# A hybrid decoder layer on one core: the last gate of the attention branch and the mask multiplications take other places in the program

## The chip, the cores and the metric

The kernel runs on one core of one Trainium2 chip. The metric is the device time of one execution in microseconds (us), as the median of several runs; lower is better. The engines are named as in the profile: PE is TensorE (matmuls; PEld its weight loads), DVE is VectorE, ACT is ScalarE, POOL is GpSimd, and SP is the queue that issues most DMAs. A name with a q behind it (ACTq, SPq) is an engine's queue that issues a DMA or handles a semaphore.

## The reference

One layer on a sequence of 1024 tokens of width 1024: a SwiGLU half-step, a mixing sub-layer with two branches, and a second SwiGLU half-step. The change lies in the mixing sub-layer:

```python
h = rms_norm(x, mix_norm[l])
z = h @ w_in[l]
q, k, v, qi, ki, wi, u, g_attn, g_pool = jnp.split(z, SPLIT_POINTS, axis=-1)
q = apply_rope(rms_norm(q.reshape(B, S, N_HEADS, HEAD_DIM), q_norm[l]), cos_h, sin_h)
k = apply_rope(rms_norm(k, k_norm[l]), cos, sin)
...
y_attn = dsa_attention(q, k, v, qi, ki, wi, topk)
y_pool = multiscale_pool(u, pool_w[l], pool_b[l], pool_scale[l])
merged = (jax.nn.sigmoid(g_attn) * (y_attn @ proj_attn[l])
          + jax.nn.sigmoid(g_pool) * (y_pool @ proj_pool[l]))
x = x + merged @ w_out[l]
```

`g_attn` and `g_pool` have 1024 channels each. The top 256 keys of a query are found by a bitwise search for the 256th largest score; what comes out is a mask over the keys, one for each block of 128 queries.

## The kernel before

Everything stands in one program in the order in which it is written; each engine works through its own part in that order and waits at semaphores for the others. Two arenas of on-chip memory, `fa` and `ra`, hold all buffers, so most operands in the profile bear these two names. PSUM is a ring of four slots (`ps()`).

**Units.** The columns of `w_in` for u, g_attn and g_pool are 20 tiles of 128 channels, "units" 0 to 19 here. `unit(u)` computes one by 48 matmuls of 512 columns (fp32 as a pair of high and low part: weight high by input high, high by low, low by high, in this order for each of eight row tiles). The weights are split on the way: ACT casts the high part (line 135), POOL subtracts it to get the low part (line 141). `next_unit(u)` runs unit u and then issues the split of unit u+2. Units 8 to 15 are the pooling branch's gates: in each turn e of that loop a unit, its sigmoid on ACT (line 995), a product of 24 matmuls, and a multiplication on DVE that reads that product from PSUM (`self.dve(... stage[e % 2] ...)`, recorded under line 119). Units 16 to 19 are gates 4 to 7 of the attention branch: `gate_out` takes the sigmoid (line 919) into a buffer and stores it to `d_gate` (line 920). For gates 4, 5 and 6 this buffer is `stage[1]`, which first has to be stored to `d_pool[7]` by the SP queue (line 1016).

**The search.** `topk()` is a generator of DVE and ACT work that is spread between the units by an estimate of the two engines' times (`pump`). At its end six masks are made, one each for query blocks 2 to 7, by four DVE instructions each (lines 865, 867, 869, 871), and ACT multiplies each mask by 1e30 (`A.mul`, lines 874 and 875). In the program's order the end of the search lies in the turns of units 14 to 17, so DVE, which lags behind, still runs it after PE has gone on.

**QKV.** Two weight tiles of 320 columns, `cd[0]` and `cd[1]`, are split inside the loop of gates 4 to 6: `cd[0]` (one cast and one subtraction of 2560 elements per row) at gate 4, `cd[1]` (1920 and 640) at gate 5. Then eight blocks follow, "N0" to "N7" here: 48 matmuls of 320 columns (`narrow`), a copy and a square on ACT (lines 1033, 1034), norm and rope on DVE and POOL (`qkv_norm`, from a reduction under line 119 to line 666), the leaving copies on ACT and POOL (`qkv_leave`, lines 1052, 1055, 1056) and a transposition on PE (`qkv_turn`, line 1062). Gate 7 (unit 19) stands behind N7. Behind it come the last `qkv_leave` and the attention loop, whose first instructions are matmuls of 128 columns on PE and an addition with a minimum on DVE for each head. DVE comes to these only when the norm of N7 is done, since that stands ahead in its order.

Of the kernel before, what the change touches and what calls it, by code (L numbers as in the profile page):

```python
# [16 lines left out]
NB = S // 128  # L17
# [10 lines left out]
BIG = 1e30  # L28
# [30 lines left out]
class Block:  # L59
# [28 lines left out]
    def f(self, kib, *shape):  # L88
        return self.cut(self.fa, self.F_END, kib, shape)
# [610 lines left out]
    def mix(self, nback):  # L700
        nc = self.nc
        A, V, P = nc.scalar, nc.vector, nc.gpsimd
# [10 lines left out]
        Ss, o = {}, 6.0  # L713
# [3 lines left out]
        Wk = f(22.5, 1024)  # L717
# [21 lines left out]
        def unit(u):  # L739
            z = self.ps()  # L740
            s = ring[u % 3]
            self.wide(z, s[:, 0], s[:, 1], self.h, ND)
            return flat(z)
# [63 lines left out]
        def topk():  # L807

            key, cand, cnt, got, least, val, up = (st[:, 6 * j:6 * j + 6] for j in range(7))
            bits = lambda t: t.bitcast(I32)
            part = lambda t, g: t[:, 3 * g:3 * g + 3]
            one = lambda t, g, k: t[:, 3 * g + k:3 * g + k + 1]
            cost = lambda b: 80 + 1.1 * 128 * (b + 1)
            n_of = lambda b: (b + 1) * 128

            def count(g, thr, op):
                for k, b in enumerate(groups[g]):  # L820
                    V.tensor_scalar(junk[0][:, 0:n_of(b)], Ss[b], one(thr, g, k) if thr is not None else 0.0, None,  # L821
                                    op0=op, op1=OP.add, accum_out=one(cnt, g, k))
                    yield cost(b)

            for k, b in enumerate(groups[0]):
                V.memset(one(least, 0, k), 2.0 * TOPK - 0.5 - n_of(b))
            V.memset(part(least, 1), TOPK - 0.5)
            for g in range(2):
                yield from count(g, None, OP.is_ge)

            V.tensor_scalar(bits(got), cnt, TOPK - 0.5, None, op0=OP.is_lt)
            V.tensor_scalar(bits(key), bits(got), 31, 31, op0=OP.logical_shift_left, op1=OP.arith_shift_right)
            V.tensor_scalar(bits(part(key, 0)), bits(part(key, 0)), -2147483648, None, op0=OP.bitwise_xor)
            yield 600
            for bit in range(30, -1, -1):
                V.tensor_scalar(bits(cand), bits(key), 1 << bit, None, op0=OP.bitwise_xor)  # L836
                for k, b in enumerate(groups[0]):
                    A.activation(junk[1][:, 0:n_of(b)], Ss[b], AF.Sign, bias=one(cand, 0, k), accum_out=one(cnt, 0, k))  # L838
                yield 400
                yield from count(1, cand, OP.is_ge)  # L840
                V.tensor_tensor(bits(got), cnt, least, op=OP.is_ge)
                V.scalar_tensor_tensor(bits(key), bits(got), bit, bits(key), op0=OP.logical_shift_left,
                                       op1=OP.bitwise_xor)
                yield 900
            V.tensor_scalar(bits(part(val, 0)), bits(part(key, 0)), -2147483648, None, op0=OP.bitwise_xor)
            V.tensor_copy(part(val, 1), part(key, 1))

            yield from count(0, val, OP.is_gt)
            v0, u0, g0 = part(val, 0), part(up, 0), part(got, 0)
            V.scalar_tensor_tensor(u0, v0, -1.0, v0, op0=OP.mult, op1=OP.max)  # L850
            V.scalar_tensor_tensor(u0, u0, 1.2 * 2.0 ** -24, v0, op0=OP.mult, op1=OP.add)
            V.tensor_scalar(bits(g0), part(cnt, 0), TOPK - 0.5, None, op0=OP.is_ge)
            V.copy_predicated(v0, bits(g0), u0)
            yield 300
            for g in (0, 1):
                yield from count(g, val, OP.is_gt)

            V.tensor_scalar(cnt, cnt, -1.0, float(TOPK), op0=OP.mult, op1=OP.add)
            for b in range(2, NB):
                g = 0 if b in groups[0] else 1  # L860
                k = groups[g].index(b)
                n = n_of(b)
                sc, eq, cum = Ss[b], junk[0][:, 0:n], junk[1][:, 0:n]
                v = one(val, g, k)
                V.tensor_scalar(eq, sc, v, None, op0=OP.is_equal)
                yield cost(b)
                V.tensor_tensor_scan(cum, eq, eq, 0.0, op0=OP.add, op1=OP.bypass)
                yield cost(b)
                V.scalar_tensor_tensor(cum, cum, one(cnt, g, k), eq, op0=OP.is_gt, op1=OP.mult)
                yield cost(b)  # L870
                V.scalar_tensor_tensor(sc, sc, v, cum, op0=OP.is_lt, op1=OP.max)
                yield cost(b)
                if b > 2:
                    A.mul(Ss[b - 1], Ss[b - 1], BIG)
            A.mul(Ss[NB - 1], Ss[NB - 1], BIG)


        u32 = [f(54, 1024), f(58, 1024)]
# [39 lines left out]
        def gate_out(e, z, buf):  # L918
            A.activation(buf, z, AF.Sigmoid)
            nc.scalar.dma_start(self.d_gate[e], buf)  # L920
            self.pump()
# [29 lines left out]
        self.split(pws[:, 0], pws[:, 1], pwraw, "pool")  # L951
        window(0)
        self.bg = topk()


        def next_unit(u):
            z = unit(u)
            split_unit(u + 2)
            return z
# [43 lines left out]
            if e == 4:  # L1003
                nc.sync.dma_start(rawCD[0], winv[:, :, 0:320])

        for e in range(4, 7):
            if e == 4:
                self.split(cd[0][0], cd[0][1], rawCD[0], "pool")
                for k, c in enumerate(parts):
                    nc.sync.dma_start(rawCD[1 + k], winv[:, c, 320:640])  # L1010
            if e == 5:
                for k, c in enumerate(parts):
                    self.split(cd[1][0][:, c], cd[1][1][:, c], rawCD[1 + k], "pool")
            z = next_unit(12 + e)
            if e == 4:
                nc.sync.dma_start(self.d_pool[held], stage[held % 2])
            gate_out(e, z, stage[1])
# [32 lines left out]
        def qkv_leave(b):  # L1050
            t1 = sets[b % 2][1]
            A.mul(qnat[:, b], t1[:, 0:8], -0.125)
            kk = t1[:, 8:9].to_broadcast([128, 2, 64])
            kb = khl[b % 2]
            A.copy(rr(kb[:, 0]), kk)
            P.tensor_tensor(kb[:, 1], kk, kb[:, 0], op=OP.subtract)
            self.split(vS[:, b, 0], vS[:, b, 1], zcd[b % 2][:, 576:640], "pool")
# [135 lines left out]
            self.pump()  # L1193
        while self.bg is not None:
            self.bg_step()
        gate_out(7, unit(19), Wk)
        qkv_leave(NB - 1)
        qkv_turn(NB - 2, quarters()[:, 0])

# [335 lines left out]
```

## Time and profile before

| | |
|---|---|
| three runs | 2055.8, 2056.26, 2056.49 us (median 2056.26) |
| the profiled execution | 2057.76 us, of which the span is 2055.9 us |
| PE busy | 1980.2 us, 96% of the span |
| DVE busy | 1455.2 us, 71% |
| ACT busy | 864.8 us, 42% |
| POOL busy | 243.2 us, 12% |

The span is the time from the first to the last instruction that the profiler recorded; the rest of the execution's time lies around it. Times within the profile count from the span's start. The part that matters lies between 1000 and 1145 us: units 16 to 18, the end of the search, N0 to N7, unit 19 and the start of attention. A row of the timeline is a run of like instructions on one engine, with its start, its length, the count, and in brackets how long the engine was idle before it and whose end released it. PE's clock has two levels here, 1.2 and 2.4 GHz; PEclk 0.50 is the lower, 1.00 the upper.

### The profile page before, as it was taken

How to read it: one execution, taken by the hardware profiler on the slowest of the kernel's cores; microseconds unless marked ns; L12 is line 12 of the kernel's file. 1: busy time of each engine (PE TensorE's matmuls, PEld its weight loads, DVE VectorE, ACT ScalarE, POOL GpSimd, SP SyncE). 2: the span in 40 equal slices, each digit the busy share in tenths (PEclk: the TensorE clock that was granted, in tenths of full speed). 3: DMA queues.
4: the chain of work that ended last, by engine and by line, in shares of the span. 5: the costliest groups of instructions: out<-in, count | busy, mean ns of one | idle time of the engine just before them, and what ended most of it. 6: DMA issues, size and time to landing. Idle time of an engine off the chain costs nothing. (4 is left out here: it accounts for less than half of the span.)

```text
span 2055.9 us, 26096 instructions
## 1 busy us (share of the span) xinstructions
PE 1980.2 (96%) x9449; PEld 1656.4 (81%) x9449; DVE 1455.2 (71%) x2464; ACT 864.8 (42%) x1437; POOL 243.2 (12%) x260
## 2 busy tenths in 40 slices
PE   8999999999999989999979898998999999999999
PEld 7788888888888877888778787787788888888887
DVE  6887777777566476788956895546787777776554
ACT  6423323333454455677423884124423323333332
POOL 0000000000000332122134654210000000000000
PEclk9999999999999999999999999999999999999999
DMA  4355454458684202022210014331255454458665
GB/s 134 103 186 183 161 167 144 164 203 313 208 274 139 67 21 72 31 92 78 76 43 11 1 51 162 137 113 53 91 181 188 158 170 144 164 200 317 194 216 173
DMA packets 167056, 287.02 MB, mean 140 GB/s; under 512 B 12160, under 2 KB 78224, under 8 KB 166928
## 3 DMA queue, kind: packets, MB, share of 16 engines
q1 hardware_dynamic: 163088, 271.73, 39.4%
q10 hardware_dynamic: 3744, 13.63, 1.7%
q8 instruction: 74, 1.21, 0.2%
q14 instruction: 54, 0.44, 0.1%
q0 software_dynamic: 96, 0.01, 0.0%
HBM read 200.91 MB, written 84.41 MB: 139 GB/s over the span
## 5 line engine op out<-in xcount | busy, mean ns | idle before, releaser
L316 PE MATMUL psum<-ra 128*128 128x512 f32 (+1 forms) x5688 | 1276.3, 386 | 11.2 <-DVE fa L502 4.3
L316 PEld LDWEIGHTS psum<-ra 128*128 128x128 f32 x5688 | 1053.9, 188 | 230.2 <-issue 5.8
L108 PE MATMUL psum<-ra 128*128 128x512 f32 (+5 forms) x3112 | 639.6, 363 | 39.0 <-POOL ra L141 12.7
L108 PEld LDWEIGHTS psum<-ra 128*128 128x128 f32 x3112 | 529.3, 191 | 128.0 <-ACT fa L795 17.4
L426 ACT CAST ra<-fa 128x512 fp32r<-128x512 f32 x280 | 168.9, 617 | 303.6 <-PE psum L316 173.6
L566 DVE TENSOR_TENSOR ra<-fa,ra 128x1024 fp32r<-128x1024 f32 x154 | 187.7, 1223 | 144.4 <-ACT ra L565 144.1
L427 DVE TENSOR_TENSOR ra<-fa,ra 128x512 fp32r<-128x512 f32 x280 | 192.2, 688 | 98.8 <-ACT ra L426 96.8
L565 ACT CAST ra<-fa 128x1024 fp32r<-128x1024 f32 x154 | 161.7, 1054 | 235.0 <-PE psum L316 214.5
L141 POOL TENSOR_TENSOR ra<-fa,ra 128x512 fp32r<-128x512 f32 (+5 forms) x56 | 102.5, 1841 | 253.9 <-ACT ra L135 245.9
L410 DVE TENSOR_TENSOR fa<-fa 128x512 f32<-128x512 f32 x160 | 109.9, 687 | 1.5
L112 PE MATMUL psum<-fa 128*128 128x128 f32 x625 | 92.4, 279 | 17.5 <-DVE ra L119 7.1
L838 ACT ACTIVATE fa<-fa 128x1024 f16<-128x1024 f32 (+2 forms) x93 | 87.1, 937 | 37.0 <-DVE fa L836 34.6
L135 ACT CAST ra<-fa 128x1024 fp32r<-128x1024 f32 (+3 forms) x72 | 60.3, 878 | 94.6 <-POOL fa L1275 78.7
L112 PEld LDWEIGHTS psum<-fa 128*128 128x128 f32 x625 | 73.1, 142 | 31.9 <-DVE ra L119 10.1
L821 DVE TENSOR_SCALAR_CACHE_REDUCE fa<-fa 128x640 f16<-128x640 f32 (+5 forms) x108 | 95.7, 886 | 3.4
L520 ACT ACTIVATE fa<-fa 128x512 f32<-128x512 f32 x60 | 37.9, 632 | 119.5 <-DVE fa L502 44.4
L119 DVE SCALAR_TENSOR_TENSOR fa<-fa 128x1024 f32<-128x1024 f32 (+7 forms) x70 | 80.2, 1155 | 6.2 <-DMA d_x<-fa 1.7
L502 DVE TENSOR_TENSOR fa<-psum,fa 128x512 f32<-128x512 f32 x80 | 55.2, 689 | 31.9 <-PE psum L316 29.8
L119 DVE TENSOR_TENSOR ra<-psum,ra 128x512 fp32r<-128x512 f32 (+4 forms) x104 | 60.7, 598 | 15.3 <-ACT ra L1144 8.3
L939 POOL MEMSET fa<- 128x256 f32 x1 | 0.3, 312 | 552.2 <-DVE fa L119 552.2
L119 DVE TENSOR_TENSOR ra<-fa,ra 128x1024 fp32r<-128x1024 f32 (+1 forms) x28 | 35.5, 1289 | 39.8 <-ACT ra L135 39.8
L541 DVE TENSOR_TENSOR fa<-fa 128x512 f32<-128x512 f32 x88 | 60.1, 683 | 2.2 <-DMA fa<-in_ffn_w_dram 2.2
(143 smaller groups left out, 1226.0 us busy)
## 6 DMA issues: line engine op xcount, KB each, us to landing
fa<-in_ffn_w_dram SPq DMA_DIRECT2D x64, 1024.0 KB, 5.6
d_a<-fa SPq DMA_DIRECT2D x154, 256.0 KB, 2.3
fa<-d_a SPq DMA_DIRECT2D x154, 256.0 KB, 3.4
d_t<-fa SPq DMA_DIRECT2D x88, 256.0 KB, 2.1
fa<-d_t SPq DMA_DIRECT2D x88, 256.0 KB, 3.8
fa<-in_ffn_w_dram SPq DMA_DIRECT2D x66, 256.0 KB, 3.9
fa<-in_w_in_dram SPq DMA_DIRECT2D x10, 1024.0 KB, 5.4
fa<-in_x_dram SPq DMA_DIRECT2D x16, 512.0 KB, 7.0
```

Of the source, the lines that this page charges most:

```text
L108: self.nc.tensor.matmul(out, rr(lhsT), rr(rhs), start=start, stop=stop)
L112: self.nc.tensor.transpose(out, in_, self.ident)
L119: fn(*a, **k)
L141: nc.gpsimd.tensor_tensor(rr(lo), src, hi, op=OP.subtract)
L316: self.nc.tensor.matmul(out, rr(lhsT), rr(rhs), start=start, stop=stop, skip_group_check=True)
L410: V.tensor_tensor(o, x, y, op=OP.subtract)
L426: A_.copy(rr(s[:, 0]), src)
L427: (V if lo_on == "dve" else nc.gpsimd).tensor_tensor(rr(s[:, 1]), src, s[:, 0], op=OP.subtract)
L565: A_.copy(rr(s[:, 0]), raws[h % 4])
L566: V.tensor_tensor(rr(s[:, 1]), raws[h % 4], s[:, 0], op=OP.subtract)
L821: V.tensor_scalar(junk[0][:, 0:n_of(b)], Ss[b], one(thr, g, k) if thr is not None else 0.0, None, op0=op, op1=OP.add, accum_out=one(cnt, g ...
L838: A.activation(junk[1][:, 0:n_of(b)], Ss[b], AF.Sign, bias=one(cand, 0, k), accum_out=one(cnt, 0, k))
```

## The change

Two edits. The multiplications of the six masks no longer follow their masks one by one; they stand in one loop behind the last mask. And gate 7 with its unit 19 leaves its place behind N7 and becomes the fourth turn of the loop of gates 4 to 6, with `stage[1]` as its buffer instead of `Wk`.

```diff
@@ topk(), the masks
                 V.scalar_tensor_tensor(sc, sc, v, cum, op0=OP.is_lt, op1=OP.max)
                 yield cost(b)
-                if b > 2:
-                    A.mul(Ss[b - 1], Ss[b - 1], BIG)
-            A.mul(Ss[NB - 1], Ss[NB - 1], BIG)
+            for b in range(2, NB):
+                A.mul(Ss[b], Ss[b], BIG)
@@ gates of the attention branch
-        for e in range(4, 7):
+        for e in range(4, 8):
             if e == 4:
                 self.split(cd[0][0], cd[0][1], rawCD[0], "pool")
@@ behind the QKV blocks
         while self.bg is not None:
             self.bg_step()
-        gate_out(7, unit(19), Wk)
         qkv_leave(NB - 1)
```

The orders of DVE, POOL and SP stay as they are; those of PE and ACT change. The lines of the changed kernel are lower by one (from the masks on) or by two (behind the QKV blocks).

On ACT, from the sigmoid of unit 15 (line 995) to the first cast of `cd[1]`, the kernel before has this row of instructions (the activations of line 874 and 875 are the mask multiplications, that of line 919 is the sigmoid of gate 4):

```order
L995 ACTIVATE fa<-psum 128x1024
L874 ACTIVATE fa<-fa 128x384
L874 ACTIVATE fa<-fa 128x512
L874 ACTIVATE fa<-fa 128x640
L874 ACTIVATE fa<-fa 128x768
L135 CAST ra<-fa 128x2560
L135 CAST ra<-fa 128x1024
L919 ACTIVATE fa<-psum 128x1024
L920 DMA d_gate<-fa 128x1024
L874 ACTIVATE fa<-fa 128x896
L875 ACTIVATE fa<-fa 128x1024
L135 CAST ra<-fa 128x1920
```

The same stretch of ACT in the changed kernel:

```order
L994 ACTIVATE fa<-psum 128x1024
L135 CAST ra<-fa 128x2560
L135 CAST ra<-fa 128x1024
L918 ACTIVATE fa<-psum 128x1024
L919 DMA d_gate<-fa 128x1024
L874 ACTIVATE fa<-fa 128x384
L874 ACTIVATE fa<-fa 128x512
L874 ACTIVATE fa<-fa 128x640
L874 ACTIVATE fa<-fa 128x768
L874 ACTIVATE fa<-fa 128x896
L874 ACTIVATE fa<-fa 128x1024
L135 CAST ra<-fa 128x1920
```

The casts of `cd[0]` and of unit 18's weights moved ahead of the first four multiplications, and those four moved behind the sigmoid of gate 4, ahead of the casts of `cd[1]` (1920, 640) and of unit 19's weights (1024).

On PE, at the change from units to QKV blocks, 48 matmuls of 512 columns (unit 19) join those ahead of N0:

```order
 L108 MATMUL psum<-ra 128x384
 L112 MATMUL psum<-fa 128x128 x10
-L108 MATMUL psum<-ra 128x512 x1160
+L108 MATMUL psum<-ra 128x512 x1208
 L108 MATMUL psum<-ra 128x320 x144
 L112 MATMUL psum<-fa 128x128 x2
```

The run of 512-column matmuls that ends with unit 18 before ends with unit 19 now; N0 to N2 (144 of 320 columns) follow it.

On PE again, behind N7 (the last 48 of 320 columns), where attention begins with the 128-column matmuls:

```order
 L112 MATMUL psum<-fa 128x128 x2
 L108 MATMUL psum<-ra 128x320 x48
-L112 MATMUL psum<-fa 128x128 x2
-L108 MATMUL psum<-ra 128x512 x48
-L112 MATMUL psum<-fa 128x128 x2
+L112 MATMUL psum<-fa 128x128 x4
 L108 MATMUL psum<-ra 128x128 x6
 L112 MATMUL psum<-fa 128x128 x2
```

Between the transposition of block 5 and that of block 6 the 48 matmuls of unit 19 are gone.

## Rows read from the trace of the kernel before

**Rows 1.** The page, busy time: us, share of the span, instructions.

```profile
PE 1980.2 (96%) x9449; PEld 1656.4 (81%) x9449; DVE 1455.2 (71%) x2464; ACT 864.8 (42%) x1437; POOL 243.2 (12%) x260
```

**Rows 2.** Timeline of PE, units 17 and 18, then N0: start, us, instructions, idle before.

```profile
1012.20 12.75 PE L108 MATMUL psum<-ra 128*128 128x512 f32 x48 [2.73 <-DVE fa L119]
1025.87 1.19 PE L108 MATMUL psum<-ra 128*128 128x512 f32 x4 [0.92 <-ACT ra L135]
1034.27 11.74 PE L108 MATMUL psum<-ra 128*128 128x512 f32 x45 [7.21 <-POOL ra L141]
1046.88 0.56 PE L108 MATMUL psum<-ra 128*128 128x320 f32 x2 [0.86 <-ACT ra L135]
1051.19 19.06 PE L108 MATMUL psum<-ra 128*128 128x320 f32 x119 [3.76 <-POOL ra L141]
```

**Rows 3.** Timeline of ACT in the same stretch.

```profile
1012.15 1.03 ACT L995 ACTIVATE fa<-psum 128x1024 f32<-128x1024 f32 x1 [18.65 <-DVE fa L119]
1013.07 1.09 ACT L874 ACTIVATE fa<-fa 128x384 f32<-128x384 f32 x2
1017.37 0.74 ACT L874 ACTIVATE fa<-fa 128x640 f32<-128x640 f32 x1 [3.20 <-DVE fa L871]
1021.80 0.85 ACT L874 ACTIVATE fa<-fa 128x768 f32<-128x768 f32 x1 [3.69 <-DVE fa L871]
1022.56 3.26 ACT L135 CAST ra<-fa 128x2560 fp32r<-128x2560 f32 x2
1041.81 1.03 ACT L919 ACTIVATE fa<-psum 128x1024 f32<-128x1024 f32 x1 [15.99 <-DMA d_pool<-fa]
1043.24 0.95 ACT L874 ACTIVATE fa<-fa 128x896 f32<-128x896 f32 x1 [0.40 <-ACT fa L919]
1045.05 3.35 ACT L135 CAST ra<-fa 128x1920 fp32r<-128x1920 f32 x3
```

**Rows 4.** Timeline of DVE: masks at the search's end, the last multiplication of `stage`, N0's norm.

```profile
1021.68 0.68 DVE L865 TENSOR_SCALAR fa<-fa 128x896 f16<-128x896 f32 x1
...
1025.65 6.37 DVE L871 SCALAR_TENSOR_TENSOR fa<-fa 128x896 f32<-128x896 f32 x1
1031.94 2.83 DVE L865 TENSOR_SCALAR fa<-fa 128x1024 f16<-128x1024 f32 x1
...
1037.01 1.20 DVE L119 TENSOR_TENSOR fa<-psum,fa 128x1024 f32<-128x1024 f32 x1
...
1039.44 1.29 DVE L871 SCALAR_TENSOR_TENSOR fa<-fa 128x1024 f32<-128x1024 f32 x1
1060.88 0.75 DVE L119 TENSOR_REDUCE fa<-fa 128x9 f32<-128x576 f32 x1 [20.15 <-ACT fa L1034]
```

**Rows 5.** Line 1016, the store of `d_pool[7]`: us from issue to landing.

```profile
DMA to landing us min/median/max: 3.5/3.5/3.5
```

**Rows 6.** Timeline of POOL: the subtractions of the split weights.

```profile
1024.95 9.26 POOL L141 TENSOR_TENSOR ra<-fa,ra 128x2560 fp32r<-128x2560 f32 x2 [28.18 <-ACT ra L135]
...
1046.90 8.07 POOL L141 TENSOR_TENSOR ra<-fa,ra 128x1920 fp32r<-128x1920 f32 x3 [12.68 <-ACT ra L135]
```

**Rows 7.** Line 1033, the copy of each QKV block's result: durations in ns, first and last start.

```profile
L1033 ACT COPY fa<-psum x8: 692/692/695, 1059.4 to 1111.3; 128x640 f32<-128x640 f32 x8
```

**Rows 8.** Timeline of DVE: the first instruction of attention.

```profile
1125.49 0.28 DVE L119 CUSTOM_DVE_ANT_0 fa<-psum,fa 128x128 f32<-128x128 f32 x1
```

**Rows 9.** Timeline of PE: N7, unit 19, the first matmuls of attention.

```profile
1103.37 7.29 PE L108 MATMUL psum<-ra 128*128 128x320 f32 x48
...
1111.15 11.18 PE L108 MATMUL psum<-ra 128*128 128x512 f32 x48
...
1122.30 0.86 PE L108 MATMUL psum<-ra 128*128 128x128 f32 x6
```

**Rows 10.** Windows of 2 us: length, busy us of PE, PEld, DVE, ACT, POOL; PEclk; DMA.

```profile
1034.00:1036.00 2.00, 1.73 (x4) 1.44 (x5) 1.97 (x2) 0.00 (x0) 0.22 (x1) 0.50 0.00 0
...
1128.00:1130.00 2.00, 0.78 (x5) 0.79 (x5) 0.53 (x4) 1.67 (x8) 1.89 (x3) 0.50 0.00 0
```

## The prediction

> **What bounds the kernel now.** I read the page's busy times first: PE works through 96% of the span [rows 1], so the reader should look for places where PE waits, and at who is late there. The timeline of PE between 1009 and 1051 us shows the largest group of such places [rows 2]: unit 17 waits 2.73 us for DVE, unit 18 waits 0.92 us for ACT and, after its first four matmuls, 7.21 us for POOL, N0 waits 0.86 us for ACT and 3.76 us for POOL. The timelines of ACT, DVE and POOL tell what lies behind these. Before unit 18, ACT holds its casts back until 1022.56, since four mask multiplications stand ahead of them and each waits for DVE's masks; POOL can start only at 1024.95 [rows 3, 6]. Before N0, another chain is late. DVE, still in the search, gets to the last multiplication of `stage` at 1037.01 and ends it at 1038.21 [rows 4]; its store lands 3.5 us later [rows 5]; the sigmoid of gate 4, which overwrites that buffer, starts at 1041.81, having waited 15.99 us for it; two multiplications follow, and the casts of `cd[1]` begin at 1045.05 [rows 3]; POOL subtracts from 1046.90 on, and N0 goes on at 1051.19 [rows 2, 6].
>
> Behind N0 the bound changes. The eight norms take DVE from 1060.88 to 1125.49 [rows 4, 8], 64.6 us or 8.1 us a block. PE delivers the blocks in (1111.3 - 1059.4) / 7 = 7.4 us each [rows 7]. So DVE's chain, not PE, sets when attention begins: N7 is done on PE at about 1110.6, unit 19 fills PE from 1111.15 to 1122.3, the first matmuls of attention follow at 1122.30 [rows 9], and DVE takes them only at 1125.49 [rows 8]. Unit 19 costs nothing where it stands; it lies wholly beside DVE's norms. Attention begins when N0 ends plus a fixed 66 us.
>
> **The multiplications.** Four of the six move from ahead of the `cd[0]` casts to behind the sigmoid of gate 4. What they free: the casts can start at 1013.2, behind the sigmoid of unit 15 (1012.15 + 1.03), instead of 1022.56 [rows 3]. POOL started 2.4 us after the casts, so it now starts at 1015.6, and with its 9.26 us it is done at 1024.9 [rows 3, 6], just when unit 17 ends (1012.20 + 12.75 = 1024.95) [rows 2]. Unit 18 follows at once, and the two waits of 0.92 and 7.21 us are gone, with the slow start behind them. But nothing downstream of unit 18 was waiting for it in a way that counts: the next wait is that of the `stage` chain, and DVE's order is the same. Unit 18 ends at about 1035.4 instead of 1046.0, and PE then waits. The gain is 0.
>
> What they cost: 1.09 + 0.74 + 0.85 = 2.7 us by their rows [rows 3]. Back to back they are shorter: the two that stood there took from 1043.24 to 1045.05, 1.81 us, of which the 896 alone shows 0.95 [rows 3], so about 0.09 overlaps at each. I take 2.4 us, bounds 2.4 and 2.7. They lie on the path, since all six have their masks by 1040.73 (1039.44 + 1.29) [rows 4] and stand between the sigmoid of gate 4 and the casts of `cd[1]`. The casts therefore start at 1045.05 + 2.4 = 1047.45.
>
> Could the `stage` chain itself move? POOL's subtractions now run from 1015.6 to 1024.9 instead of 1024.95 to 1034.2, beside other masks. In the trace DVE lost time beside them: the mask of 896 took 6.37 us where the larger one of 1024 took 1.29, and the next instruction 2.83 where the smaller 896 took 0.68 [rows 4]; that is about 5.2 + 2.1 = 7.3 us. DVE has no idle time there, so the loss comes earlier but is the same in sum. No row shows it beside the masks of 640 and 768. The bounds are no loss at all (the chain 7.3 us earlier) and the whole of POOL's 9.26 us (2.0 us later); I take no shift, since the same kinds of instructions meet, and the ends are wide on purpose.
>
> The Trainium skill bears on this place: SBUF — State Buffer, Who interferes with whom, says that GpSimd and a VectorE instruction with two SBUF inputs exclude each other for a whole instruction, and that the order of issue decides who blocks. The rows of the slow mask agree with the first half; no row here shows VectorE going first beside so long a subtraction. By the second half VectorE could go first this time; that is rival A below.
>
> **Unit 19.** It now runs between unit 18 and N0, and its weights are split behind `cd[1]`. ACT's three casts take 3.35 us [rows 3], so its high part is there at 1050.8, and the first four matmuls run then. POOL starts 1.85 us after the first cast (1046.90 - 1045.05) [rows 3, 6], so at 1049.3, and needs 8.07 us for the three subtractions, of which unit 19's is the last [rows 6]: 1057.4. Until then PE waits, though the weights of N0 are ready sooner, because unit 19 stands ahead in PE's order. The rest of unit 19 is what unit 18 was in the kernel before, a start after such a wait: there the clock showed 0.50, the 1.2 GHz level [rows 10], and 45 recorded matmuls took 11.74 us [rows 2]. Unit 19 in its old place, at full clock, took 11.18 us for 48, so some 10.4 for as many as these [rows 9]. I take 11.74, to 1069.1. Then N0 runs at full clock like N7, 7.2 us (7.29 with the end of the last) [rows 9], to 1076.3. Before, it ended at 1059.43 [rows 7]. N0 is late by **16.9 us**.
>
> What the move gives back: 11 us of PE behind N7. There DVE is later than PE anyway. N7 now ends on PE at about 1076.3 + 51.9 = 1128.2 (seven blocks at 7.4) [rows 7], DVE's norms end at 1125.49 + 16.9 = 1142.4, and PE waits the difference out. The transposition of block 6 and the first heads' matmuls need only block 6's norm, a block earlier, so they are ready before DVE is. Gain 0. PE starts attention after a longer wait; but the clock stood at 0.50 there before too [rows 10], so I add nothing, with 0 to 2 us as bounds. The sigmoids of gates 5, 6 and 7 share `stage[1]` and wait for one another's stores; they run on ACT inside unit 19's and N0's time, and nothing of N0's waits for them but one place in ACT's order, before the copy of N0. The one of gate 7 runs at 1069, 7 us ahead of that copy. Cost 0.
>
> **Sum.** The whole of the delay reaches attention and, since nothing behind it starts by the clock on the wall, the end. The profiled execution took 2057.76 us for its span of 2055.9, 1.5 us more than the median; the sum is a difference, so I put it on the median: 2056.26 + 16.9 = **2073.2 us**. By bounds: 1.3 less if unit 19 runs at full clock, 0.3 more for the multiplications, 2 more or a little less for DVE's loss, 0 to 2 more for attention's start, so 2071 to 2077.5 with all of one sign; they rarely are.
>
> **Rivals.** A: DVE loses nothing beside POOL this time. Then the `stage` chain is 7.3 us earlier and N0 late by 9.6 us only: 2065.9 us. If instead POOL has to wait until DVE has finished at 1040.73 - 7.3 = 1033.4, its 9.26 us end at 1042.7, unit 18 runs from then some 11.7 us, and unit 19 starts at 1054.4: at full clock it ends at 1065.4 and N0 at 1072.6, late by 13.2 us: 2069.5. For it speaks that other instructions meet; against it, that both of the instructions that met the subtractions were slow. 10%.
>
> B, on the other side: the weights of unit 19 are ready when unit 18 ends, so that PE runs 17, 18, 19 and N0 without a wait, and the filled gap of 8.1 us counts. Unit 18 would end at 1035.4, unit 19 at 1046.4 and N0 at 1053.6, 5.8 us earlier than before: 2050.5 us. It decides at the sigmoid of gate 4: from its start to unit 19's low weights there are 1057.4 - 1041.81 = 15.6 us, so it would have to start by 1019.8 for all of this, 22 us earlier. It breaks even when unit 19 starts at 1041.2, 16 us earlier than I have it. DVE's order with the search ahead of `stage` speaks against it [rows 4]; for it speaks only that PE is busy 96% of the span, the view by which any PE gap looks like a loss. 5%.
>
> C: the delay is made good in attention or the delay is half hidden, so that the time stays within 0.2%, which is 4 us and about what a measurement of this kernel can tell from no change. That needs PE, not DVE, to set the norms' pace, 7.4 against 8.1 us a block: 8 blocks give back 5.6 us at most, not 12. 4%.
>
> That the change does nothing of what it says is no rival, since the order of the built program shows both edits.
>
> **How the numbers follow.** The forecast has 77%, A 10%, B 5%, C 4%, a delay of more than 21 us 4%. Faster by over 0.2%: B, 5%. Within 0.2%: C, 4%. Slower: 91%. The forecast's own 2071 to 2077.5 holds some 7 in 10; with A, from 2065.5 to 2077.5, it is over 8 in 10.
>
> **What would show it.** In the changed kernel's timeline of PE, unit 18 follows unit 17 without a wait, at about 1025; then PE waits about 15 us, runs four matmuls, waits some 6.5 us more for POOL, and runs 44 of 512 columns to 1069. On ACT the sigmoid of gate 4 still waits for `d_pool` until about 1041.8 and six multiplications follow it in a row. The copy of N0 starts at 1076, the first instruction of attention on DVE at 1142, 8.1 us a block between. If the sigmoid of gate 4 starts near 1034, A is right; if it starts near 1020, B. If the copies of N0 and the first instruction of attention do not move by the same amount, the claim that DVE's chain is fixed is wrong, and with it the last step.

## The result and the profile after

The changed kernel takes 2072.74 us (four runs, 2071.55 to 2075.09) against 2056.3 us for the kernel before, run beside it: ratio 1.0083, 95% interval 1.0068 to 1.0097. It is slower by 16.4 us. The profiled execution took 2075.09 us, with a span of 2073.3 us.

The page's busy times of the changed kernel answer to [rows 1]:

```profile
PE 1982.5 (96%) x9449; PEld 1659.0 (80%) x9449; DVE 1455.0 (70%) x2464; ACT 865.0 (42%) x1437; POOL 242.4 (12%) x260
```

Every engine does the same work in the same number of instructions, so the time went into waiting. The timeline of PE in the changed kernel shows where, as start, length, instructions and the wait ahead [rows 2]:

```profile
1013.52 22.24 PE L108 MATMUL psum<-ra 128*128 128x512 f32 x96 [2.79 <-DVE fa L119]
1051.60 2.08 PE L108 MATMUL psum<-ra 128*128 128x512 f32 x4 [15.84 <-ACT ra L135]
1058.14 27.15 PE L108 MATMUL psum<-ra 128*128 128x512 f32 x143 [4.47 <-POOL ra L141]
```

Units 17 and 18 run as one piece of 96 matmuls: the waits of 0.92 and 7.21 us are gone. In their place stands one of 15.84 us, four matmuls of unit 19, and one of 4.47 us. The last row runs on through N0 and N1 into N2. This execution came to unit 17 at 1013.52, that of before at 1012.20, so 1.3 us of the two spans' difference lie ahead of the change.

The timeline of ACT answers to [rows 3]:

```profile
1013.47 1.03 ACT L994 ACTIVATE fa<-psum 128x1024 f32<-128x1024 f32 x1 [18.68 <-DVE fa L119]
1014.39 3.28 ACT L135 CAST ra<-fa 128x2560 fp32r<-128x2560 f32 x2
1042.68 1.02 ACT L918 ACTIVATE fa<-psum 128x1024 f32<-128x1024 f32 x1 [25.01 <-DMA d_pool<-fa]
...
1044.11 4.18 ACT L874 ACTIVATE fa<-fa 128x384 f32<-128x384 f32 x6 [0.40 <-ACT fa L918]
1048.20 3.35 ACT L135 CAST ra<-fa 128x1920 fp32r<-128x1920 f32 x3
...
1070.81 1.03 ACT L918 ACTIVATE fa<-psum 128x1024 f32<-128x1024 f32 x1 [14.60 <-PE psum L108]
...
1077.85 0.69 ACT L1032 COPY fa<-psum 128x640 f32<-128x640 f32 x1 [6.01 <-PE psum L108]
```

The casts of `cd[0]` and of unit 18 now start at 1014.39, right behind the sigmoid of unit 15. The sigmoid of gate 4 waits for the store of `d_pool[7]` as before (25.01 us instead of 15.99, since ACT comes to it earlier). Behind it the six multiplications take 4.09 us to the next cast, where two took 1.81. The sigmoid of gate 7 at 1070.81 marks the end of unit 19, the copy at 1077.85 that of N0.

DVE in the changed kernel, the same stretch and the first instruction of attention [rows 4, 8]:

```profile
1016.85 6.34 DVE L869 SCALAR_TENSOR_TENSOR fa<-fa 128x640 f16<-128x640 f16 x1
1023.23 2.90 DVE L871 SCALAR_TENSOR_TENSOR fa<-fa 128x640 f32<-128x640 f32 x1
...
1038.49 1.20 DVE L119 TENSOR_TENSOR fa<-psum,fa 128x1024 f32<-128x1024 f32 x1
...
1143.79 0.28 DVE L119 CUSTOM_DVE_ANT_0 fa<-psum,fa 128x128 f32<-128x128 f32 x1
```

And POOL's subtractions [rows 6]:

```profile
1016.80 8.64 POOL L141 TENSOR_TENSOR ra<-fa,ra 128x2560 fp32r<-128x2560 f32 x2 [18.71 <-ACT ra L135]
1050.05 8.04 POOL L141 TENSOR_TENSOR ra<-fa,ra 128x1920 fp32r<-128x1920 f32 x3 [24.61 <-ACT ra L135]
```

The same events of the two profiled executions, cut into four pieces:

| piece, us | before | after | difference |
|---|---|---|---|
| start to unit 17's first matmul | 1012.20 | 1013.52 | +1.3 |
| unit 17 to the copy of N0 | 47.2 | 64.3 | **+17.1** |
| copy of N0 to attention's first instruction on DVE | 66.1 | 65.9 | -0.1 |
| from there to the end of the span | 930.4 | 929.5 | -0.9 |

The whole loss lies between unit 17 and N0.

### The profile page after: what moved, and what is told of

The parts are those of the page before. It is cut to its first block, busy times and chain, and to the rows that moved or that the text cites. A ratio compares the mean times of both kernels' runs of the same rounds, so it can differ in the third digit from the quotient of the medians.

```text
span 2073.3 us, 26095 instructions
## 1 busy us (share of the span) xinstructions
PE 1982.5 (96%) x9449; PEld 1659.0 (80%) x9449; DVE 1455.0 (70%) x2464; ACT 865.0 (42%) x1437; POOL 242.4 (12%) x260
## 5 line engine op out<-in xcount | busy, mean ns | idle before, releaser
L108 PE MATMUL psum<-ra 128*128 128x512 f32 (+5 forms) x3112 | 637.1, 362 | 47.0 <-ACT ra L135 17.1
```

Source lines behind the costliest of these rows:

```text
L108: self.nc.tensor.matmul(out, rr(lhsT), rr(rhs), start=start, stop=stop)
```

## The experiments

Nine kernels in three groups, each group with runs of the kernel before beside it. The time of before was 2056.65 us beside the first four, 2056.91 beside the next four and 2056.23 beside the last; ratios and differences are against these.

**e1_muls_only: only the multiplications in a row.**

```diff
-                if b > 2:
-                    A.mul(Ss[b - 1], Ss[b - 1], BIG)
-            A.mul(Ss[NB - 1], Ss[NB - 1], BIG)
+            for b in range(2, NB):
+                A.mul(Ss[b], Ss[b], BIG)
```

> The kernel before with the mask multiplications in a row behind the search; gate 7 stays behind N7. My theory (DVE's norms behind N0 set when attention begins): unit 18 starts without a wait, N0 ends 2.4 us later because four more multiplications stand ahead of the casts of cd[1], and so does everything behind it: 2058.7 us (2057.5 to 2059.5). Rival B (PE's idle time is what counts): the gap of 8 us ahead of unit 18 is filled and the time falls to about 2048 us.

Measured: 2059.45 us, ratio 1.0012 (1.0003 to 1.0022), 2.8 us more. The timeline of PE in this kernel, units 17 and 18, then N0:

```profile
1012.33 22.24 PE L108 MATMUL psum<-ra 128*128 128x512 f32 x96 [2.76 <-DVE fa L119]
1038.56 0.63 PE L108 MATMUL psum<-ra 128*128 128x320 f32 x1 [3.99 <-DVE fa L119]
1048.85 0.90 PE L108 MATMUL psum<-ra 128*128 128x320 f32 x2 [9.65 <-ACT ra L135]
1053.17 23.35 PE L108 MATMUL psum<-ra 128*128 128x320 f32 x141 [3.42 <-POOL ra L141]
```

The gap ahead of unit 18 is gone, and three waits of 17 us in sum stand ahead of N0 instead of two of 4.6 us. N0's main part starts at 1053.17 instead of 1051.19. Filling PE's gap gained nothing that shows beside the 2.3 us that the multiplications cost, and rival B's 2048 us is out.

**e2_gate_only: only gate 7 moved.**

```diff
-        for e in range(4, 7):
+        for e in range(4, 8):
...
-        gate_out(7, unit(19), Wk)
```

> The kernel before with gate 7 moved into the loop of the other gates; the multiplications stay one by one. My theory: unit 18 ends at 1046 as before, the casts of cd[1] begin at 1045.05 as before, unit 19's low weights are ready at 1055.0, its body runs cold for 11.7 us, N0 ends at 1073.9 instead of 1059.4: 14.5 us more, 2070.8 us (2069 to 2073). Together with the 2.4 us of the multiplications that is the whole change. Rival: the loss comes from the multiplications, and moving unit 19 is neutral, since it is the same PE work in another place: 2056 to 2058 us.

Measured: 2070.37 us, ratio 1.0065 (1.0048 to 1.0082), 13.7 us more. With the 2.8 of e1 that is 16.5, and the whole change costs 16.4. PE in this kernel, units 18 and 19:

```profile
1034.72 12.10 PE L108 MATMUL psum<-ra 128*128 128x512 f32 x44 [7.22 <-POOL ra L141]
1048.28 1.19 PE L108 MATMUL psum<-ra 128*128 128x512 f32 x4 [1.47 <-ACT ra L135]
1054.83 30.46 PE L108 MATMUL psum<-ra 128*128 128x512 f32 x168 [5.36 <-POOL ra L141]
```

Unit 18 waits as before; unit 19's body starts at 1054.83, where the expectation had 1055.0.

**e3_stage0: the changed kernel, its sigmoids in a buffer that is free sooner.**

```diff
-            gate_out(e, z, stage[1])
+            gate_out(e, z, stage[0])
```

> The changed kernel with the sigmoids of gates 4 to 7 in stage[0], whose store to d_pool[6] is done by about 1016 us, instead of stage[1]. My theory (the chain through stage[1] delays the casts of cd[1] and of unit 19's weights): the sigmoid of gate 4 starts at about 1016 to 1018; the multiplications then wait for their masks, the last ends at about 1041.8; casts from there, unit 19's low weights at 1051.7, its body to 1063.4, N0 to 1070.6: 5.7 us less than the changed kernel, 2067.0 us (2065.5 to 2069). Rival (the store is not what delays ACT, DVE's masks or POOL are): 2072 to 2073 us.

Measured: 2068.81 us, ratio 1.0056 (1.0041 to 1.0071), 12.2 us above before, where the changed kernel was 16.4 above. The expected gain of 5.7 us came as 4.2. ACT in this kernel, gate 4's sigmoid, the last multiplication, the casts of `cd[1]`:

```profile
1016.35 1.02 ACT L918 ACTIVATE fa<-psum 128x1024 f32<-128x1024 f32 x1
...
1041.04 1.06 ACT L874 ACTIVATE fa<-fa 128x1024 f32<-128x1024 f32 x1 [5.67 <-DVE fa L871]
1042.00 3.35 ACT L135 CAST ra<-fa 128x1920 fp32r<-128x1920 f32 x3
...
1065.21 1.03 ACT L918 ACTIVATE fa<-psum 128x1024 f32<-128x1024 f32 x1 [15.20 <-PE psum L108]
```

The sigmoid no longer waits for the store, and the casts come at 1042.00 instead of 1048.20. The chain through the store is real; the last mask on DVE is late right behind it, so only part of the wait goes. In the trace the missing 1.5 us of the expected gain are unit 19's own: its body took 13.3 us, from 1051.95 to gate 7's sigmoid at 1065.21, where 11.7 were expected.

**e4_short19: the kernel before, with unit 19 cut to 6 of its 48 matmuls.**

```diff
-        gate_out(7, unit(19), Wk)
+        zs = self.ps()
+        self.wide(zs, ring[1][:, 0], ring[1][:, 1], self.h, 1)
+        gate_out(7, flat(zs), Wk)
```

> The kernel before with unit 19 cut to the first of its eight row tiles (6 matmuls instead of 48; 42 are left out, so gate 7 is computed from an eighth of its input). My theory (unit 19 behind N7 lies wholly beside DVE's norms): no gain, 2056.3 us, up to 2058 if PE's clock is lower when attention begins. Rival B or C (PE sets when attention begins): 42 matmuls by 0.23 us, 9.6 us less, 2046.7 us.

Measured: 2056.93 us, ratio 1.0001 (0.9992 to 1.0011). 42 matmuls less, and nothing gained. PE behind N7 in this kernel:

```profile
1110.76 1.64 PE L108 MATMUL psum<-ra 128*128 128x512 f32 x6
1118.08 1.01 PE L112 MATMUL psum<-fa 128*128 128x128 f32 x2 [5.68 <-ACT fa L1055]
1118.75 1.52 PE L108 MATMUL psum<-ra 128*128 128x128 f32 x6
1126.02 1.00 PE L112 MATMUL psum<-fa 128*128 128x128 f32 x2 [5.76 <-ACT fa L1055]
```

and the first instruction of attention on DVE:

```profile
1125.04 0.28 DVE L119 CUSTOM_DVE_ANT_0 fa<-psum,fa 128x128 f32<-128x128 f32 x1
```

PE waits 5.68 and 5.76 us for the keys that DVE has yet to norm, and DVE comes to attention at 1125.04, as it did at 1125.49 with the whole unit [rows 8]. The place behind N7 was free for unit 19.

**e6_double19: the kernel before, with unit 19 computed twice there.**

```diff
+        unit(19)
         gate_out(7, unit(19), Wk)
```

> The kernel before with unit 19 computed twice behind N7 (the first result is not used). My theory: it lies beside DVE's norms until DVE is done, 3.2 us after unit 19's end; of the 10.6 to 11 us that a second one takes, 7.5 to 8 us come out of the end, 2064.3 us (2062.5 to 2066). Rival (all PE work there counts): 2067.5 us. Rival (cover without end): 2056.5 us.

Measured: 2065.45 us, ratio 1.0044 (1.0029 to 1.0058), 8.5 us more, with 6 to 12 us in the interval. PE in this kernel, the two units and where attention begins:

```profile
1110.31 22.06 PE L108 MATMUL psum<-ra 128*128 128x512 f32 x96
1132.21 0.38 PE L112 MATMUL psum<-fa 128*128 128x128 f32 x2
1135.12 0.89 PE L108 MATMUL psum<-ra 128*128 128x128 f32 x6 [2.53 <-ACT ra L1062]
```

and DVE's first instruction there:

```profile
1135.71 0.29 DVE L119 CUSTOM_DVE_ANT_0 fa<-psum,fa 128x128 f32<-128x128 f32 x1 [10.96 <-PE psum L108]
```

Now DVE waits 10.96 us for PE: the cover has an end, and one unit fits it while a second does not. DVE was done with the norms at 1124.75 (1135.71 - 10.96), and the two units end on PE at 1132.37. So of the second unit's 11.0 us, 7.6 came out behind DVE, as the 7.5 to 8 of the expectation, and 3.4 lay beside the norms; that speaks against the rival that all of it counts, which the time alone does not put out. The copy of N0 came at 1058.61, so attention began 77.1 us behind it, 11.0 more than before: the other 3.3 us lie between the units' end and DVE's start. 2.5 of them are a new wait that the expectation had not: PE stands for the copy of block 6's transposed keys (line 1062), which ACT makes only behind gate 7's sigmoid. Rival "cover without end" is out.

**e5_split_order: the changed kernel, unit 19's weights split ahead of `cd[1]`.**

```diff
-            if e == 5:
+            if e == 6:
                 for k, c in enumerate(parts):
                     self.split(cd[1][0][:, c], cd[1][1][:, c], rawCD[1 + k], "pool")
```

> The changed kernel with the splits of cd[1] and of unit 19's weights exchanged: unit 19's at gate 5, cd[1]'s at gate 6. My theory (unit 19 holds N0 up since its weights are split behind cd[1]): its high part is ready one cast behind the multiplications, at about 1048.5, its low part at 1050.8; its body runs cold for 11.7 us to 1062.5; cd[1] is ready before that, at 1057; N0 ends at 1069.7 instead of 1076.3, 6.6 us less than the changed kernel: 2066.1 us (2064.5 to 2068). Rival (N0 waits for its own weights, unit 19 fills a gap that is there anyway): 2072 to 2073 us.

Measured: 2065.17 us, ratio 1.0044 (1.0029 to 1.0059), 8.3 us above before, 8.1 below the changed kernel's 16.4, where 6.6 were expected. In the traces N0's copy comes 7.3 us sooner behind unit 17 (57.1 against 64.3 us). PE in this kernel, unit 19:

```profile
1046.83 2.07 PE L108 MATMUL psum<-ra 128*128 128x512 f32 x4 [12.12 <-ACT ra L135]
1049.28 32.90 PE L108 MATMUL psum<-ra 128*128 128x512 f32 x188 [0.38 <-POOL ra L141]
```

Unit 19's wait for POOL shrinks from 4.47 to 0.38 us, and N0 follows without a wait. About half of the loss was that unit 19 stood last in the split queue while it stood first in PE's.

**b1_muls_late: the kernel before, the multiplications behind N7.**

```diff
-                if b > 2:
-                    A.mul(Ss[b - 1], Ss[b - 1], BIG)
-            A.mul(Ss[NB - 1], Ss[NB - 1], BIG)
...
         while self.bg is not None:
             self.bg_step()
+        for b in range(2, NB):
+            A.mul(Ss[b], Ss[b], BIG)
         gate_out(7, unit(19), Wk)
```

> The kernel before with all six mask multiplications behind the eight QKV blocks, on ACT, which waits there for the norm of N7; gate 7 stays behind N7. My theory (what stands between gate 4's sigmoid and the casts of cd[1] is on the path, what stands on ACT behind N7 is not): the casts begin 1.8 to 2.2 us earlier than before, so does all behind: 2054.5 us (2053.5 to 2056). Rival (the filled gap ahead of unit 18 is what counts): 2048 us. Rival (the multiplications on ACT delay attention): 2058 to 2061 us.

Measured: 2055.93 us, ratio 0.9996 (0.9987 to 1.0006). The expected gain of 1.8 us lies inside the interval, and so does none: inconclusive on the gain. Both rivals, 8 us less and 2 to 5 us more, are out. The gap ahead of unit 18 is filled here as in e1, with no multiplication left on the path, so this is the cleaner test of what the gap is worth: at most 2.7 us with the multiplications' own gain.

**b3_late_stage0_mult7: b1, with the sigmoids in stage[0] and the last multiplication of `stage` ahead of the masks.**

```diff
+            self.paused = e == 7
             self.dve(1024, V.tensor_tensor, stage[e % 2], flat(z2), sg, op=OP.mult)
+            self.paused = False
...
-            gate_out(e, z, stage[1])
+            gate_out(e, z, stage[0])
```

> As the last one, with the gates' sigmoids in stage[0] and with the last multiplication of stage ahead of the masks in DVE's order (the search pauses for it). My theory (the chain through DVE's order, the store and ACT holds N0 back): unit 18 follows unit 17 and N0 follows unit 18, N0 ends at about 1043; then DVE, with the subtractions of cd[1] beside the search too, ends the search at 1045 to 1049 and sets the beginning of the norms; attention begins 11 to 15 us earlier than before: 2043 us (2041 to 2047). Rival (PE's 11 us of unit 19 come back as soon as DVE is earlier, or the norms become slower): 2050 to 2054 us.

Measured: 2045.61 us, ratio 0.9948 (0.9931 to 0.9965). It beats the kernel before by 11.3 us, and the changed one by 27 (by the medians of different runs). PE in this kernel:

```profile
1010.77 44.72 PE L108 MATMUL psum<-ra 128*128 128x512 f32 x240 [2.80 <-DVE fa L119]
```

and DVE:

```profile
1011.77 1.22 DVE L119 TENSOR_TENSOR fa<-psum,fa 128x1024 f32<-128x1024 f32 x1 [1.15 <-ACT fa L992]
...
1014.36 6.02 DVE L865 TENSOR_SCALAR fa<-fa 128x640 f16<-128x640 f32 x1
1020.42 3.58 DVE L867 TENSOR_TENSOR_SCAN fa<-fa 128x640 f16<-128x640 f16 x1
1024.03 4.77 DVE L869 SCALAR_TENSOR_TENSOR fa<-fa 128x640 f16<-128x640 f16 x1
1028.83 2.07 DVE L871 SCALAR_TENSOR_TENSOR fa<-fa 128x640 f32<-128x640 f32 x1
1030.83 2.75 DVE L865 TENSOR_SCALAR fa<-fa 128x768 f16<-128x768 f32 x1
...
1046.86 1.28 DVE L871 SCALAR_TENSOR_TENSOR fa<-fa 128x1024 f32<-128x1024 f32 x1
1048.06 0.75 DVE L119 TENSOR_REDUCE fa<-fa 128x9 f32<-128x576 f32 x1
```

From unit 17 through N2 PE runs without a recorded wait. The last multiplication of `stage` is done at 1013 instead of 1038, N0 is no longer late, and DVE goes from its last mask straight into the norm of N0: the search's end is the new bound, at 1048. How the 11.3 us divide among the three edits is not shown: b1 alone is inconclusive, stage[0] alone brought 4.2 us in the changed kernel (e3), and the moved multiplication was not run alone.

**e7_gate_on_b3: the last kernel, with gate 7 moved as in the change.** The diff on it is that of e2.

> The fast reordering (multiplications behind N7, sigmoids in stage[0], the last multiplication of stage ahead of the masks) with gate 7 moved into the loop of the other gates as in the change. My theory: unit 19's weights are now split by 1033, before unit 18 ends at 1034.4, so unit 19 runs without a wait and warm for 10.8 us, N0's copy comes at 1052 instead of 1041.4; DVE, which ends its search at 1048, then waits for N0 until 1053.5 instead of not at all: 5.5 us more than that reordering, 2051.1 us (2049.5 to 2053). So the same move costs 14 us in the kernel before and 5.5 here. Rival (unit 19 ahead of N0 always costs its whole run on the path): 2056 to 2057 us. Rival (with no wait on PE the place of unit 19 does not matter): 2045 to 2046.5 us.

Measured: 2051.68 us, ratio 0.9977 (0.9967 to 0.9986), 6.1 us above b3 by the two medians (2045.61 was taken beside a before of 2056.91, so 6.8 by the differences). The interval, 2049.4 to 2053.4 us, leaves out both rivals. PE in this kernel:

```profile
1010.70 51.55 PE L108 MATMUL psum<-ra 128*128 128x512 f32 x260 [2.80 <-DVE fa L119]
```

and DVE at the norm of N0:

```profile
1053.76 0.75 DVE L119 TENSOR_REDUCE fa<-fa 128x9 f32<-128x576 f32 x1 [5.69 <-ACT fa L1033]
```

PE does not wait at all here, unit 19 runs at once behind unit 18, and the move still costs the 5.7 us by which N0 is later than DVE. So the loss has two parts: what unit 19 waits, and that it runs ahead of N0 at all.

## Why the prediction was right

**What bounds the stretch.** The claim was that DVE's norms, not PE, set when attention begins. It holds: 65.9 us from N0's copy to attention against 66.1 before, with unit 19 in one place or the other; e4 takes 42 matmuls out of the place behind N7 and gains nothing. The same distance is 65.9 to 66.1 us in the traces of e1 to e5, b1 and e7 too. It is longer only in e6, where PE is late, and in b3, where the norms start late behind the search; from their start it is 64.5 us there, as 64.6 before. The chain is not DVE's alone: in each block DVE stands idle for some 1.5 us until POOL has done its part of the rope (line 665), so the 8.1 us a block belong to the two engines together.

**The filled gap is worth 0.** Unit 18 ended 10 us sooner, and e1, where only that and the multiplications changed, lost 2.8 us; in b1 the gap is filled too and no multiplication is on the path, and the time stays within 2.7 us less and 1.2 us more.

**The multiplications.** Predicted 2.4 us on the path, in the trace 4.09 - 1.81 = 2.3 us, and 2.8 us in e1's time (interval 0.6 to 4.5 us).

**The stage chain.** It was taken as unmoved. DVE's loss beside POOL did come earlier and with the same sum: the masks of 640 show 6.34 and 2.90 us where both took 0.89 before, 7.5 us in all, against 7.3 at the other masks before. Rival A, which needed DVE to lose nothing, is out. The Trainium skill (SBUF — State Buffer, Who interferes with whom) has GpSimd and a VectorE instruction with two SBUF inputs exclude each other; the mask of line 869 has two such inputs and agrees. What differed is the store: it landed in 2.9 us, as the store's line in the changed kernel shows,

```profile
DMA to landing us min/median/max: 2.9/2.9/2.9
```

0.6 us less than before [rows 5]. From unit 17 to gate 4's sigmoid it is 29.2 us against 29.6. The change did not make the store faster: it landed in 2.8 or 2.9 us in e1, e2, e4, e5, e6 and b1 as well and in 3.3 in e3, so the 3.5 us that the prediction read were the longest of these.

In one reading of the rows the prediction was wrong. It said that no row shows VectorE going first beside so long a subtraction; one row of the kernel before does, the third instruction of the mask of 896:

```profile
1024.46 1.15 DVE L869 SCALAR_TENSOR_TENSOR fa<-fa 128x896 f16<-128x896 f16 x1
```

It was under way when POOL began at 1024.95 [rows 6] and kept its 1.15 us. POOL's two subtractions took 9.26 us there, and 9.26 to 9.28 in e2, e4 and e6, which meet the same instruction; in the changed kernel, e1, e3, e5 and b1, where POOL starts just ahead of DVE's instruction, they took 8.64 or 8.65. So the 0.6 us more are probably POOL's own wait; no run was made to show it.

**Unit 19.** Its first four matmuls at 1051.60 and its body at 1058.14 were forecast at 1050.8 and 1057.4, and this execution was 1.3 us late when it came here. (The forecast 6.5 us between the two hold the four matmuls' own 2.08 us; the wait itself is 4.47.) The mis-sized term is its body: 11.74 us were taken, and it took 12.7 (1058.14 to the sigmoid at 1070.81). The clock in the changed kernel, in windows of 2 us (columns as in [rows 10]), shows why, beside that of the kernel before at the unit that served as the model. Before:

```profile
1036.00:1038.00 2.00, 2.00 (x8) 1.53 (x8) 2.00 (x2) 0.00 (x0) 0.00 (x0) 0.72 0.00 0
1038.00:1040.00 2.00, 2.00 (x10) 1.67 (x9) 1.97 (x3) 0.00 (x0) 0.00 (x0) 1.00 0.48 190
```

After:

```profile
1058.00:1060.00 2.00, 1.85 (x4) 1.50 (x5) 0.00 (x0) 0.00 (x0) 0.09 (x1) 0.50 0.17 70
1060.00:1062.00 2.00, 2.00 (x6) 1.60 (x5) 0.00 (x0) 0.00 (x0) 0.00 (x0) 0.50 0.00 0
1062.00:1064.00 2.00, 2.00 (x7) 1.59 (x7) 0.00 (x0) 0.00 (x0) 0.00 (x0) 0.69 0.00 0
1064.00:1066.00 2.00, 2.00 (x10) 1.65 (x10) 0.00 (x0) 0.00 (x0) 0.00 (x0) 1.00 0.00 0
```

PE stayed at the 1.2 GHz level until after 1062, with 0.50 in the first two windows, and was back at 1.00 by 1064, less than 6 us after its start. The unit that served as the model, also starting after a wait, at 1034.27, was back at 1.00 by 1038, less than 4 us after its start. The two errors, the store's and this one's, are of opposite sign and under 1 us each.

**The sum.** Predicted 16.9 us; 17.1 in the traces between unit 17 and N0's copy, 16.4 in the medians. e1 and e2 split it into 2.8 and 13.7 where the steps had 2.4 and 14.5; both steps lie inside the intervals of these runs (0.6 to 4.5 and 9.9 to 16.9 us). Rival B (2050.5 us) and C are out: unit 19's weights were not there when unit 18 ended, and attention gave nothing back.

**Attention's start.** PE waited long there, as forecast, and had its first matmuls ready in time. In the changed kernel's timeline:

```profile
1136.84 1.02 PE L112 MATMUL psum<-fa 128*128 128x128 f32 x2 [7.07 <-ACT fa L1054]
1137.51 1.52 PE L108 MATMUL psum<-ra 128*128 128x128 f32 x6
```

They end at 1139.0, and DVE takes the first at 1143.79.

## What to carry to other kernels

A gap on the busiest engine is worth filling only if what comes behind it is waiting for that engine; here another engine's chain ended later, and filling the gap moved the wait. Work that fills a later engine's time for free (unit 19 behind N7) should be left there, and cutting it short shows whether it is free. When a wait is long, follow it back to the last instruction that is late for no need of its own (here one multiplication behind a search in DVE's order) and take that out of the way. In b3 that was worth 11 us, together with another buffer for the sigmoids and with the mask multiplications behind N7, where moving the waiting engine's work cost 16; the runs do not tell what each of the three brought.

## What the runs showed of the hardware

The time that a run of subtractions on POOL takes from DVE was nearly the same in the two places seen: 7.3 us beside the masks of 896 and 1024 elements, 7.5 us beside those of 640, out of 9.26 and 8.64 us of POOL's work. In b3 five subtractions in a row, 19.13 us of POOL's work, stretched five of DVE's instructions by 14.8 us in sum, a scan among them (3.58 us where the same scan took 1.49 in the changed kernel), and the search ended at 1048 instead of 1041, so such a shift is not free once the search is the bound. And the cost of starting PE after a wait varied: 44 or so matmuls of 512 columns took 11.74 us in one execution, 12.10 in another, 12.7 in a third and 13.3 in e3 (the last two up to the sigmoid behind them), whose granted clock was 0.50 until 1058, 6 us after the start at 1051.95.
